# GpSimd's share of the weight splits, the context squares of the first norm, and the pieces of the first modulation weights in a two-layer block

## The chip, the cores and the metric

The kernel runs on one core of a Trainium2 chip. The metric is the time of one execution on the device in microseconds; the median of several runs counts. A core has five engines that work in parallel on instruction streams of their own: TensorE (PE in the profile; its weight loads are PEld), VectorE (DVE), ScalarE (ACT), GpSimd (POOL) and SyncE (SP). SP, ACT and POOL also issue DMA transfers; SPq, ACTq and POOLq are those queues.

## What is computed

A block of two layers over 512 tokens of 1024 channels (`x`) and 256 context tokens (`ctx`). Each layer has three parts: a half feed-forward network, a mixer, another half feed-forward network. Every part normalises its input, modulates it with terms computed from a condition vector `c`, and adds its gated output to the residual.

```python
def rms_norm(x, g):
    xf = x.astype(jnp.float32)
    y = xf * lax.rsqrt(jnp.mean(jnp.square(xf), axis=-1, keepdims=True) + EPS)
    return (y * g.astype(jnp.float32)).astype(x.dtype)
def modulate(x, g, shift, scale):
    return rms_norm(x, g) * (1.0 + scale) + shift
def swiglu(h, w_in, w_out):
    a, b = jnp.split(h @ w_in, 2, axis=-1)
    return (jax.nn.silu(a) * b) @ w_out
def macaron_half_ffn(x, g, shift, scale, gate, w_in, w_out):
    return x + 0.5 * gate * swiglu(modulate(x, g, shift, scale), w_in, w_out)
```

The mixer of layer 0 combines neighbourhood attention and an mLSTM, that of layer 1 is a spatial gating unit. The context takes part in layer 0 up to its mixer. `w_mod` holds, for each layer, nine modulation terms as 1024 x 1024 matrices. All of it is float32.

## The kernel before

Channels lie on the 128 partitions: `xT` is 128 x 8 x 512, eight channel tiles (k = 0 to 7) of 512 tokens, and `cT` the same for the context. To reach float32 accuracy with TensorE's faster format, each operand of a large product is split into a high and a low half, and a product is three matmuls: high by high, low by high, high by low.

**The weight stream.** All large weights come through one `Stream` object, `W`, in the order of use, 128 x 1024 tiles numbered from 0. `load` starts the transfer `raw` on SP, in a ring of three buffers. `prep` lets ScalarE cast `raw` to the high half `whi` (L83) and subtracts to get the low half `wlo` (L84), four buffers each. The subtraction, called the split here, runs on VectorE, except for the tile numbers in the set `W.pool`, which go to GpSimd:

```python
(nc.gpsimd if i in self.pool else nc.vector).tensor_tensor(lo, r, hi.bitcast(F32), ALU.subtract)
...
W.pool.update(range(6))
for i in mark:
    W.pool.update(range(i - 4, i + 4))
```

`mark` holds the tile numbers at which one part ends and the next begins, so the set has the first six tiles and four on either side of five hand-overs: 62 to 69, 98 to 105, 164 to 171, 230 to 237 and 278 to 285, 46 in all.

**The hand-overs.** They are numbered 1 to 5 here: feed-forward 00 to mixer, mixer to feed-forward 01, 01 to 10, 10 to gating, gating to 11 (first digit the layer, second the part). The last products of a part (`pl...`) go in two halves of 256 tokens. Each adds its tile to the residual (L306, VectorE); ScalarE squares it (`sq`, L229) and VectorE adds the square to `nacc` (L230). After eight tiles TensorE sums `nacc` over the partitions (`st_x`), ScalarE takes the root (`nr_x`, L239) and loads a table ahead of the next function (L215), VectorE takes the reciprocal (L242), TensorE broadcasts it (`bc_x`), and for each k VectorE makes `nt` (L255), ScalarE the high half `hx..h` (L256) and VectorE the low half `hx..l` (L257) of the next part's input. The first products of the next part (`pa`, `pb`) follow k by k. Names carry the part: `hx10l` and `nacc_x10` belong to feed-forward 10, the context's are `hc`, `nacc_c`, `st_c`.

**The start.** Feed-forward 00 can't begin before its modulation terms are there. `load_mod` fetches 1 MB for each k (`wmk`, L572) as four transfers, in which a piece of 512 bytes goes to each place; `mod_products` multiplies it with the condition (`pm`), VectorE copies the result (`mr`, L616), `mod_columns` turns it into columns (`pcol`) and computes gain `G` and shift `S`, and `modulated` makes `hx00` for this k (L637 to L639), which `x_products` uses (`st`). The norm of `x` is `norm_start` (squares on ScalarE, seven adds into `sacc` on VectorE, L596), and it is called a second time, for the context, at k = 4 of the loop, ahead of `x_products(4)`. Behind the loop `ctx_modulated` makes `hc00` for the context (L643 to L645) and `ctx_products` uses it (`stc`).

**Work in the background.** The modulation terms needed later are not products but sums on VectorE: `mod_task` loads 512 KB (`wm`, L153) by GpSimd's queue into a ring of three buffers, and VectorE accumulates (`macc`, L159 the first, L161 the rest), for the first terms twice per load, once for each condition vector. `mp0`, which holds these buffers, takes the place in memory of the start's tiles.

**What sets the order.** The program is written in Python with a library that gives each engine one instruction stream, worked off in order; the library moves instructions against the written order by the dependencies, by the buffers of its tile pools (an instruction that reuses a buffer waits for the last reader) and by its own estimate of when a result is ready. `gtiles` gives out the buffers of the gated activations `gx` and `gc`; `spacer` is a tile with a small memset on GpSimd that shifts what comes behind it in memory.

Of the kernel before, what the change touches and what calls it, by code (L numbers as in the profile page):

```python
# [37 lines left out]
def block_kernel(ctx: ExitStack, tc: tile.TileContext, T: dict, out: bass.AP, stop: str = ""):  # L38
    nc = tc.nc
# [55 lines left out]
    W = Stream()  # L95
# [335 lines left out]
    def ffn(l, s, cur, nxt, gxf, gcf, bgsteps, side, first=None, left=0):  # L431
        nm = f"{l}{s}"
        hx, hc = cur.hx, cur.hc
        bgn[0] = bgsteps
        nslot = 6 if hc else 8
        gx = gc = None
        with tc.tile_pool(name=f"g{nm}", bufs=1, side=side, reuse_waits="tile") as gp:
            def glu(pa, pb, n, gh, gl, nme):
                sl = gp.tile([P, 512], F32, tag="silu", name=f"sl{nme}", bufs=2)[:, :n]
                nc.scalar.activation(halved(sl), inorder(pa), AF.Silu)  # L440
                nc.vector.tensor_tensor(halved(sl), halved(sl), inorder(pb), ALU.mult)  # L441
                nc.scalar.copy(gh, sl)
                last = nc.vector.tensor_tensor(gl, sl, gh.bitcast(F32), ALU.subtract)
                if not hc:
                    pace[0] = last

            def gtiles(f):
                e = f % nslot if hc or f < 18 else f"z{f}"
                if not hc and f == 18:
                    spacer(gp, 192, f"padz{nm}")  # L450
                g = [gp.tile([P, 512], F32R, tag=f"gx{e}{i}", name=f"gx{nm}{f}{i}") for i in range(2)]
                if hc:
                    if f < nslot:
                        spacer(gp, 192, f"padgc{f}")
                    g += [gp.tile([P, 256], F32R, tag=f"gc{e}{i}", name=f"gc{nm}{f}{i}") for i in range(2)]
                    if f < nslot:
                        spacer(gp, 64, f"padge{f}")
                if not hc and f == NF - 1:
                    spacer(gp, 64, f"padze{nm}")
                return g  # L460

            gs = {f: gtiles(f) for f in range(2)}
            if first:
                for f in range(2):
                    pab, pc = first[f]
                    glu(pab[0], pab[1], 512, gs[f][0], gs[f][1], f"st{f}")
                    glu(pc[:, :256], pc[:, 256:], 256, gs[f][2], gs[f][3], f"stc{f}")
            else:
                us = list(zip(*[[W.next(), W.next()] for hf in range(2)]))
            for t0, t1 in () if first else HALVES:  # L470
                for f in range(2):
                    pab = bank(f"pa{nm}{f}{t0}"), bank(f"pb{nm}{f}{t0}")
                    for k in range(KD):
                        if (t0, f) == (0, 0) and k in (5, 7):
                            cur.go()
                        for ab in range(2):
                            w = pick(us[f][k // 4], slice(None), k % 4, slice(ab * P, (ab + 1) * P))
                            product(pab[ab][:, :256], w, pick(hx, slice(None), k, slice(t0, t1)), k == 0, k == 7)
                    glu(pab[0][:, :256], pab[1][:, :256], 256, gs[f][0][:, t0:t1], gs[f][1][:, t0:t1], f"{nm}{f}{t0}")
            bg.step(2 * bgsteps)  # L480
            for kind, f in ffn_order(l, s):
                if kind == "o":
                    if gx is None:
                        bg.finish()
                        gx, gc = gxf(), gcf() if hc else None
                    out_op(f"{nm}{f[0]}", [gs.pop(i) for i in range(*f)], (f[1] - f[0]) // 4, gx, gc)
                elif f > 1:
                    u = [W.next(), W.next()]
                    g = gs[f] = gtiles(f)
                    pab = bank(f"pa{nm}{f}"), bank(f"pb{nm}{f}")  # L490
                    pc = bank(f"pc{nm}{f}") if hc else None
                    for hf in range(2):
                        for ab in range(2):
                            for kk in range(4):
                                k = hf * 4 + kk
                                w = pick(u[hf], slice(None), kk, slice(ab * P, (ab + 1) * P))
                                x = pick(hx, slice(None), k)
                                if hc:
                                    product2(pab[ab], pc[:, ab * 256:(ab + 1) * 256], w, x, pick(hc, slice(None), k),
                                             k == 0, k == 7, k == 0 and ab == 0, k == 7 and ab == 1)  # L500
                                else:
                                    product(pab[ab], w, x, k == 0, k == 7)
                    glu(pab[0], pab[1], 512, g[0], g[1], f"{nm}{f}")
                    if hc:
                        glu(pc[:, :256], pc[:, 256:], 256, g[2], g[3], f"{nm}{f}c")
                    bg.step(bgsteps)
            bg.need(left)
            cur.close()
            nxt.open()
            out_c(f"{nm}c", [gs[16], gs[17]], gx, gc)  # L510
            out_last(f"{nm}l", [gs[i] for i in range(18, NF)], gx, nxt, gc)
# [11 lines left out]
    mark = []  # L523
# [23 lines left out]
    mark.append(len(W.aps))  # L547
    stream_ffn(1, 1)
    W.pool.update(range(6))
    for i in mark:  # L550
        W.pool.update(range(i - 4, i + 4))


    cpool = ExitStack()
# [4 lines left out]
    sp = spx.enter_context(tc.tile_pool(name="sp", bufs=1, side="right"))  # L559
# [7 lines left out]
    def load_mod(i):  # L567
        k0, k1 = MODK[i]
        t = sp.tile([P, KD, 2, (k1 - k0) * P], F32, tag="wmk", name=f"wmk{i}", bufs=5)
        for h in range(2):  # L570
            for j in range(2):
                nc.sync.dma_start(t[:, 4 * h:4 * h + 4, j], T["w_mod"][0, 512 * h:512 * h + 512, j * D + k0 * P:j * D + k1 * P]  # L572
                                  .rearrange("(k p) c -> p k c", p=P))
        wmk.append(t)

    for k in range(0, KD, 2):
# [9 lines left out]
        load_mod(i)  # L586
    warm(AF.Sqrt, cs[:, 0, 0:1])

    def norm_start(nn, n):
        st = aux(f"sts{n}")  # L590
        acc = sp.tile([P, N], F32, tag="sacc", name=f"sacc{n}", bufs=1)[:, :n]
        for k in range(KD):
            sq = sp.tile([P, N], F32, tag="ssq", name=f"ssq{n}{k}", bufs=4)[:, :n] if k else acc
            nc.scalar.activation(sq, nn.x[:, k], AF.Square)
            if k:
                nc.vector.tensor_tensor(acc, acc, sq, ALU.add)  # L596
        for c in range(n // P):
            mm(st[:, 2 * c:2 * c + 2], acc[:, c * P:(c + 1) * P], ones, True, True)
        r = tp.tile([P, 8], F32, tag="nrs", name=f"nrs{n}", bufs=1)[:, :n // 64]
        nc.scalar.activation(r, st[:, :n // 64], AF.Sqrt, bias=epst, scale=1.0 / D)  # L600
        if n == NCX:
            warm(AF.Silu, r[:, 0:1])
        nc.vector.reciprocal(r, r)
        bc = aux(f"bcx{n}")
        for c in range(n // P):
            mm(bc[:, c * P:(c + 1) * P], r[:, 2 * c:2 * c + 1].to_broadcast([P, P]), ident, True, True)
        return bc[:, :n]
# [12 lines left out]
    for k in range(5):  # L620
        mm(junk, ones[:, 0:1].to_broadcast([P, P]), xT[:, k], True, True)
    mrs = {0: mod_products(0)}
    bcx = norm_start(s00.nx, N)
    xn = sp.tile([P, KD, N], F32, name="xn")
    s00.open()

    def start():
# [44 lines left out]
        def x_products(k):  # L672
            for f in range(2):
                for ab in range(2):
                    w = pick(us[f][k // 4], slice(None), k % 4, slice(ab * P, (ab + 1) * P))
                    product(pab[f][ab], w, pick(hx, slice(None), k), k == 0, k == 7)
# [642 lines left out]
def layout(i):  # L1319
    a = {}  # L1320
    a["xT"] = i["x"][0].T.reshape(KD, P, N).transpose(1, 0, 2)
    a["cT"] = i["ctx"][0].T.reshape(KD, P, NCX).transpose(1, 0, 2)
    a["cc"] = np.stack([i["c"][0], i["c_ctx"]]).reshape(2, KD, P).transpose(2, 0, 1)
    a["w_mod"] = i["w_mod"]
    a["b_mod"] = i["b_mod"].reshape(2, 9, KD, P).transpose(3, 0, 1, 2)
    a["norm_g"] = i["norm_g"].reshape(2, 3, KD, P).transpose(3, 0, 1, 2)
    a["final_g"] = i["final_g"].reshape(KD, P).T
# [74 lines left out]
```

## Time and profile before

| | |
|---|---|
| median of three runs | 2307.08 us (2306.27 to 2308.08) |
| the profiled execution | 2307.41 us |
| its span in the trace | 2305.6 us, so 1.8 us around it |
| TensorE busy | 2246.3 us, 97% of the span |
| VectorE, ScalarE, GpSimd busy | 56%, 34%, 11% |
| splits on VectorE / on GpSimd | 302 / 46 |

Times are in microseconds from the start of the span. A row of a group names source line, engine, operation and tiles with buffer numbers left out, how often it occurs, its busy time and the mean of one in nanoseconds, and the idle time of that engine ahead of it with what ended it. A row of the timeline has start, duration, engine, line and operation; several equal instructions in a row are merged (x3), their duration being that from the first start to the last end. PEclk is TensorE's granted clock as a share of its full one; 0.50 is its level of 1.2 GHz, 1.00 that of 2.4 GHz.

### The profile page before, as it was taken

The numbers are of one execution on the slowest core, as the hardware profiler recorded it, in microseconds if no ns is written. First come the engines' busy times: TensorE is split into PE (matmuls) and PEld (weight loads), VectorE is DVE, ScalarE is ACT, GpSimd is POOL, SyncE is SP. The second block draws the span as 40 slices with busy tenths as digits, with TensorE's granted clock in tenths as the row PEclk, the third lists the DMA queues.
The fourth block names the chain that finished last, engine by engine and source line by source line (L and its number), as shares of the span: only waits on it lengthen the run. The fifth ranks groups of instructions, "written<-read, shape, count | busy, mean of one in ns | idle before, by whom it ended". The sixth has DMA issues, their size and how long they took to land.

```text
span 2305.6 us, 31899 instructions
## 1 busy us (share of the span) xinstructions
PE 2246.3 (97%) x12926; PEld 1989.7 (86%) x12926; DVE 1284.2 (56%) x2045; ACT 779.7 (34%) x1283; POOL 262.8 (11%) x300
## 2 busy tenths in 40 slices
PE   7999999999999999999999999999999999999998
PEld 4999999999878977888888898888878888988887
DVE  5996653327556447766574766433536756433336
ACT  3322122124354356532323432322335424323222
POOL 2212120002030033100010301000300003000000
PEclk8999999999999989999999999999999999999999
DMA  8566561221122231165564356333242322333231
GB/s 268 175 201 196 167 185 65 70 68 52 63 83 65 65 119 62 65 210 192 173 211 155 111 174 210 101 101 101 92 146 93 99 92 74 101 100 108 94 110 65
DMA packets 95347, 281.33 MB, mean 122 GB/s; under 512 B 11024, under 2 KB 29632, under 8 KB 94816
## 3 DMA queue, kind: packets, MB, share of 16 engines
q1 hardware_dynamic: 69648, 196.18, 25.7%
q0 software_dynamic: 22960, 77.99, 11.3%
q10 hardware_dynamic: 2592, 5.13, 0.7%
q8 instruction: 101, 1.65, 0.3%
q14 instruction: 46, 0.38, 0.1%
HBM read 274.95 MB, written 6.00 MB: 122 GB/s over the span
## 4 chain that ended last, share of the span: by engine, by line
PE 88%; DVE 6%; issue 3%; ACT 1%; DMA 1%; POOL 0%; ACTq 0%; DVEq 0%; POOLq 0%
PE pa L108 19%; PE pb L108 19%; PE po L108 14%; PE pc L108 4%; PE su L108 4%; PE sv L108 4%; PE posg L108 3%; PE poc L108 2%; PE O L108 1%; PE tva L108 1%; PE nS L108 1%; PE st L108 1%; PE pomx L108 1%; PE fqa L108 1%; PE pl11l L108 1%
## 5 line engine op out<-in xcount | busy, mean ns | idle before, releaser
L83 ACT CAST whi<-raw 128x1024 fp32r<-128x1024 f32 x348 | 364.8, 1049 | 919.1 <-PE pb L108 330.4
L84 DVE TENSOR_TENSOR wlo<-raw,whi 128x1024 fp32r<-128x1024 f32 x302 | 370.1, 1226 | 399.6 <-ACT whi L83 383.7
L108 PE MATMUL po<-gx,whi 128*128 128x512 f32 x1024 | 305.4, 380 | 0.0
L441 DVE TENSOR_TENSOR sl<-sl,pb 128x512 f32<-128x512 f32 (+1 forms) x92 | 60.0, 652 | 272.0 <-PE pb L108 182.1
L108 PEld LDWEIGHTS po<-gx,whi 128*128 128x128 f32 x1024 | 183.7, 189 | 24.0
L108 PE MATMUL po<-gx,wlo 128*128 128x512 f32 x512 | 194.4, 380 | 0.0
L84 POOL TENSOR_TENSOR wlo<-raw,whi 128x1024 fp32r<-128x1024 f32 (+1 forms) x46 | 109.8, 2388 | 598.7 <-ACT whi L83 585.1
L161 DVE SCALAR_TENSOR_TENSOR macc<-wm,cs,macc 128x1024 f32<-128x1024 f32 x133 | 168.3, 1280 | 10.5 <-DMA wm<-in_w_mod 9.4
L153 POOL DMA_DIRECT2D wm<-in_w_mod x128 | 68.1, 532 | 573.9 <-DVE macc L161 368.7
L306 DVE SCALAR_TENSOR_TENSOR xT<-po,gate,xT 128x512 f32<-128x512 f32 x80 | 59.8, 748 | 95.9 <-PE po L108 95.8
L440 ACT ACTIVATE sl<-pa 128x512 f32<-128x512 f32 (+1 forms) x92 | 52.3, 569 | 174.3 <-PE pa L108 174.3
L108 PEld LDWEIGHTS po<-gx,wlo 128*128 128x128 f32 x512 | 97.2, 190 | 10.2
L108 PE MATMUL pc<-hc00l,whi 128*128 128x256 f32 x320 | 88.0, 275 | 0.0
L108 PE MATMUL pc<-hc00h,whi 128*128 128x256 f32 x320 | 87.3, 273 | 0.0
L108 PE MATMUL pc<-hc00h,wlo 128*128 128x256 f32 x320 | 87.2, 273 | 0.0
L108 PE MATMUL pa<-hx12l,whi 128*128 128x512 f32 (+1 forms) x192 | 70.5, 367 | 3.1 <-DVE hx12l L257 3.1
L108 PE MATMUL pa<-hx10l,whi 128*128 128x512 f32 (+1 forms) x192 | 70.2, 366 | 3.1 <-DVE hx10l L257 3.1
L108 PE MATMUL pa<-hx02l,whi 128*128 128x512 f32 (+1 forms) x192 | 70.2, 366 | 2.8 <-DVE hx02l L257 2.8
L108 PE MATMUL pa<-hx02h,whi 128*128 128x512 f32 (+1 forms) x192 | 70.3, 366 | 0.1
L108 PE MATMUL pa<-hx12h,whi 128*128 128x512 f32 (+1 forms) x192 | 70.3, 366 | 0.0
L108 PE MATMUL pa<-hx10h,whi 128*128 128x512 f32 (+1 forms) x192 | 70.1, 365 | 0.0
L108 PE MATMUL pa<-hx12h,wlo 128*128 128x512 f32 (+1 forms) x192 | 70.0, 365 | 0.0
(561 smaller groups left out, 5893.6 us busy)
## 6 DMA issues: line engine op xcount, KB each, us to landing
raw<-in_ffn_in SPq DMA_DIRECT2D x176, 512.0 KB, 3.3
wm<-in_w_mod POOLq DMA_DIRECT2D x128, 512.0 KB, 4.6
raw<-in_ffn_out SPq DMA_DIRECT2D x64, 512.0 KB, 3.3
raw<-in_mix_in SPq DMA_DIRECT2D x26, 512.0 KB, 3.2
wmk<-in_w_mod SPq DMA_DIRECT2D x32, 256.0 KB, 5.4
raw<-in_ffn_last SPq DMA_DIRECT2D x16, 512.0 KB, 3.3
raw<-in_sg_v SPq DMA_DIRECT2D x16, 512.0 KB, 3.4
raw<-in_sg_u SPq DMA_DIRECT2D x16, 512.0 KB, 3.5
```

The source lines that it names most:

```text
L83: nc.scalar.copy(hi, r)
L84: (nc.gpsimd if i in self.pool else nc.vector).tensor_tensor(lo, r, hi.bitcast(F32), ALU.subtract)
L108: lastmm[0] = nc.tensor.matmul(o, lhsT, rhs, start=start, stop=stop)
L153: ins = nc.gpsimd.dma_start(wt, T["w_mod"][l, k * P:(k + 1) * P, j * D:(j + 1) * D])
L161: nc.vector.scalar_tensor_tensor(acc[v], wt, cs[:, v, k:k + 1], acc[v], ALU.mult, ALU.add)
L306: nc.vector.scalar_tensor_tensor(xs, inorder(o), g[:, k:k + 1], xs, ALU.mult, ALU.add)
L440: nc.scalar.activation(halved(sl), inorder(pa), AF.Silu)
L441: nc.vector.tensor_tensor(halved(sl), halved(sl), inorder(pb), ALU.mult)
```

## The change

There are four edits. `W.pool` keeps only the first six tiles; the 40 splits around the hand-overs run on VectorE. `norm_start` is taken apart: `square_start` does one square and one add on a given engine. The norm of `x` calls it with VectorE as before; the context's eight squares are now written two at a time at k = 3 to 6 of the loop, with their adds on GpSimd, and its `norm_start` at k = 6 behind `x_products(6)`. The host lays out the first modulation weights as `w_mod0`, so that `load_mod` makes two transfers of 512 KB per k, with 4 KB in one piece, instead of four of 256 KB. And `gtiles` has neither spacers nor buffers of their own for the steps from 18 on.

```diff
             def gtiles(f):
-                e = f % nslot if hc or f < 18 else f"z{f}"
-                if not hc and f == 18:
-                    spacer(gp, 192, f"padz{nm}")
+                e = f % nslot
...
-                    if f < nslot:
-                        spacer(gp, 192, f"padgc{f}")
...
     W.pool.update(range(6))
-    for i in mark:
-        W.pool.update(range(i - 4, i + 4))
...
         for h in range(2):
-            for j in range(2):
-                nc.sync.dma_start(t[:, 4 * h:4 * h + 4, j], T["w_mod"][0, 512 * h:512 * h + 512, j * D + k0 * P:j * D + k1 * P]
-                                  .rearrange("(k p) c -> p k c", p=P))
+            nc.sync.dma_start(t[:, 4 * h:4 * h + 4], T["w_mod0"][k0, h])
...
+    sacc = {}
+
+    def square_start(nn, n, k, eng):
+        if k == 0:
+            sacc[n] = sp.tile([P, N], F32, tag="sacc", name=f"sacc{n}", bufs=1)[:, :n]
+        sq = sp.tile([P, N], F32, tag="ssq", name=f"ssq{n}{k}", bufs=4)[:, :n] if k else sacc[n]
+        nc.scalar.activation(sq, nn.x[:, k], AF.Square)
+        if k:
+            eng.tensor_tensor(sacc[n], sacc[n], sq, ALU.add)
+
+    def norm_start(n):
         st = aux(f"sts{n}")
-        acc = sp.tile([P, N], F32, tag="sacc", name=f"sacc{n}", bufs=1)[:, :n]
-        for k in range(KD):
-            sq = sp.tile([P, N], F32, tag="ssq", name=f"ssq{n}{k}", bufs=4)[:, :n] if k else acc
-            nc.scalar.activation(sq, nn.x[:, k], AF.Square)
-            if k:
-                nc.vector.tensor_tensor(acc, acc, sq, ALU.add)
+        acc = sacc[n]
...
         for k in range(KD):
-            if k == 4:
-                bc = norm_start(s00.nc, NCX)
             x_products(k)
+            if 3 <= k < 7:
+                for i in range(2 * k - 6, 2 * k - 4):
+                    square_start(s00.nc, NCX, i, nc.gpsimd)
+            if k == 6:
+                bc = norm_start(NCX)
```

What this moves on the engines is seen at three places. First VectorE at hand-over 3, the end of the first half's modulation; the numbers at the ends of names tell tiles apart (`pl01l07256` is channel tile 7 of the second half, `sq_x10_7_256` its square). Before:

```order
L257 SCALAR_TENSOR_TENSOR hx10l_11681<-nt_x10_0_7_12023,mod_1_0_0_9945,hx10h_11680 128x256
L230 TENSOR_TENSOR nacc_x10_256_11937<-nacc_x10_256_11937,sq_x10_4_256_12045 128x256
L306 SCALAR_TENSOR_TENSOR xT_82<-pl01l06256_12065,gate_0_2_0_10025,xT_82 128x256
L230 TENSOR_TENSOR nacc_x10_256_11937<-nacc_x10_256_11937,sq_x10_5_256_12062 128x256
L306 SCALAR_TENSOR_TENSOR xT_82<-pl01l07256_12082,gate_0_2_0_10025,xT_82 128x256
L230 TENSOR_TENSOR nacc_x10_256_11937<-nacc_x10_256_11937,sq_x10_6_256_12079 128x256
L230 TENSOR_TENSOR nacc_x10_256_11937<-nacc_x10_256_11937,sq_x10_7_256_12096 128x256
L242 RECIPROCAL nr_x10_256_12166<-nr_x10_256_12166 128x4
```

The same place on VectorE after:

```order
L257 SCALAR_TENSOR_TENSOR hx10l_11637<-nt_x10_0_7_11979,mod_1_0_0_9905,hx10h_11636 128x256
L230 TENSOR_TENSOR nacc_x10_256_11893<-nacc_x10_256_11893,sq_x10_5_256_12018 128x256
L306 SCALAR_TENSOR_TENSOR xT_82<-pl01l07256_12038,gate_0_2_0_9985,xT_82 128x256
L230 TENSOR_TENSOR nacc_x10_256_11893<-nacc_x10_256_11893,sq_x10_6_256_12035 128x256
L84 TENSOR_TENSOR wlo170_12064<-raw170_11726,whi170_12063 128x1024
L230 TENSOR_TENSOR nacc_x10_256_11893<-nacc_x10_256_11893,sq_x10_7_256_12052 128x256
L84 TENSOR_TENSOR wlo171_12070<-raw171_11732,whi171_12069 128x1024
L242 RECIPROCAL nr_x10_256_12122<-nr_x10_256_12122 128x4
```

Two splits now stand around the last sum; two more (`wlo168`, `wlo169`) stand ahead of the first reciprocal and behind the first `nt`.

Second, GpSimd at the start of feed-forward 00. Before, without the memsets in between:

```order
L84 TENSOR_TENSOR wlo3_247<-raw3_140,whi3_246 128x1024
...
L153 DMA wm0_2_0_792<-in_w_mod 128x1024
L153 DMA wm0_2_1_798<-in_w_mod 128x1024
L84 TENSOR_TENSOR wlo4_253<-raw4_242,whi4_252 128x1024
L84 TENSOR_TENSOR wlo5_259<-raw5_244,whi5_258 128x1024
L153 DMA wm0_2_2_802<-in_w_mod 128x1024
```

GpSimd after; the seven adds of the context's squares stand where the dots are:

```order
L84 TENSOR_TENSOR wlo3_231<-raw3_132,whi3_230 128x1024
...
L84 TENSOR_TENSOR wlo4_237<-raw4_226,whi4_236 128x1024
L84 TENSOR_TENSOR wlo5_243<-raw5_228,whi5_242 128x1024
L153 DMA wm0_2_0_768<-in_w_mod 128x1024
L153 DMA wm0_2_1_774<-in_w_mod 128x1024
L153 DMA wm0_2_2_778<-in_w_mod 128x1024
```

All loads of `wm0_2` moved behind the two splits.

Third, VectorE a little later, from the first gating product of `st`; `macc0_2_0` and `macc0_2_1` are the sums for the two condition vectors. Before:

```order
L443 TENSOR_TENSOR gx0001_757<-slst0_772,gx0000_756 128x512
L159 TENSOR_SCALAR macc0_2_0_794<-wm0_2_0_792,cs_84 128x1024
L159 TENSOR_SCALAR macc0_2_1_796<-wm0_2_0_792,cs_84 128x1024
L161 SCALAR_TENSOR_TENSOR macc0_2_0_794<-wm0_2_1_798,cs_84,macc0_2_0_794 128x1024
L161 SCALAR_TENSOR_TENSOR macc0_2_1_796<-wm0_2_1_798,cs_84,macc0_2_1_796 128x1024
L84 TENSOR_TENSOR wlo6_819<-raw6_250,whi6_818 128x1024
L441 TENSOR_TENSOR slstc0_777<-slstc0_777,stc0_268 128x256
```

After, from the last of the six gating products on:

```order
L443 TENSOR_TENSOR gc0011_747<-slstc1_763,gc0010_746 128x256
L161 SCALAR_TENSOR_TENSOR macc0_2_1_772<-wm0_2_1_774,cs_84,macc0_2_1_772 128x1024
L161 SCALAR_TENSOR_TENSOR macc0_2_0_770<-wm0_2_2_778,cs_84,macc0_2_0_770 128x1024
...
L161 SCALAR_TENSOR_TENSOR macc0_2_0_770<-wm0_2_5_790,cs_84,macc0_2_0_770 128x1024
L161 SCALAR_TENSOR_TENSOR macc0_2_1_772<-wm0_2_5_790,cs_84,macc0_2_1_772 128x1024
L84 TENSOR_TENSOR wlo6_795<-raw6_234,whi6_794 128x1024
L84 TENSOR_TENSOR wlo7_801<-raw7_240,whi7_800 128x1024
```

`wlo6` stood behind four accumulations and stands behind twelve.

## Rows read from the trace of the kernel before

**Rows 1.** The page's part 4: the chain that ended last, by engine.

```profile
PE 88%; DVE 6%; issue 3%; ACT 1%; DMA 1%; POOL 0%; ACTq 0%; DVEq 0%; POOLq 0%
```

**Rows 2.** Waits of TensorE: product, what it waited for: us in total, times, longest.

```profile
PE st_x L108 <- DVE nacc_x L230: 12.2, 5, 4.2
...
PE pa L108 <- DVE hx10l L257: 3.1, 3, 1.3
...
PE pcol L108 <- DVE mr L616: 2.7, 1, 2.7
```

**Rows 3.** Busy time by stretch: PE, PEld, DVE, ACT, POOL, then PEclk, DMA share, GB/s.

```profile
560.00:590.00 30.00, 23.94 (x168) 23.32 (x168) 23.33 (x43) 14.38 (x30) 10.11 (x9) 0.83 0.29 94
955.00:975.00 20.00, 15.11 (x112) 14.16 (x111) 15.84 (x35) 9.66 (x22) 6.73 (x8) 0.91 0.43 158
1310.00:1330.00 20.00, 14.92 (x111) 14.12 (x110) 15.60 (x34) 9.57 (x21) 5.00 (x5) 0.91 0.24 79
1665.00:1690.00 25.00, 18.71 (x75) 15.12 (x74) 15.63 (x35) 10.71 (x22) 4.24 (x3) 0.86 0.54 190
1940.00:1960.00 20.00, 14.95 (x98) 14.15 (x97) 14.17 (x30) 8.90 (x19) 4.93 (x3) 0.83 0.25 80
```

**Rows 4.** The same view, two stretches behind idle time, at the start and hand-over 3.

```profile
43.30:50.10 6.80, 5.73 (x26) 3.10 (x27) 2.79 (x11) 0.81 (x1) 0.00 (x0) 0.50 0.66 257
...
1323.30:1326.70 3.40, 3.40 (x19) 3.40 (x18) 0.87 (x3) 1.57 (x4) 0.00 (x0) 0.50 0.00 0
```

**Rows 5.** Timelines at hand-over 3, of GpSimd, VectorE and ScalarE.

```profile
1310.39 2.35 POOL L84 TENSOR_TENSOR wlo<-raw,whi 128x1024 fp32r<-128x1024 f32 x1 [0.23 <-ACT whi L83]
...
1303.62 2.23 DVE L230 TENSOR_TENSOR nacc_x<-nacc_x,sq_x 128x256 f32<-128x256 f32 x1
...
1306.79 0.43 DVE L230 TENSOR_TENSOR nacc_x<-nacc_x,sq_x 128x256 f32<-128x256 f32 x1 [0.55 <-ACT sq_x L229]
...
1308.70 4.72 DVE L257 SCALAR_TENSOR_TENSOR hx10l<-nt_x,mod,hx10h 128x256 fp32r<-128x256 f32 x3
...
1314.86 1.26 DVE L257 SCALAR_TENSOR_TENSOR hx10l<-nt_x,mod,hx10h 128x256 fp32r<-128x256 f32 x3
...
1321.21 0.43 DVE L230 TENSOR_TENSOR nacc_x<-nacc_x,sq_x 128x256 f32<-128x256 f32 x1 [0.21 <-ACT sq_x L229]
...
1322.62 1.28 ACT L215 ACT_TABLE_LOAD   x1
```

**Rows 6.** The page's costliest groups: the splits on VectorE and on GpSimd.

```profile
L84 DVE TENSOR_TENSOR wlo<-raw,whi 128x1024 fp32r<-128x1024 f32 x302 | 370.1, 1226 | 399.6 <-ACT whi L83 383.7
...
L84 POOL TENSOR_TENSOR wlo<-raw,whi 128x1024 fp32r<-128x1024 f32 (+1 forms) x46 | 109.8, 2388 | 598.7 <-ACT whi L83 585.1
```

**Rows 7.** Timeline at the start: GpSimd, VectorE, TensorE around the copy of `mr4`.

```profile
37.87 2.37 POOL L84 TENSOR_TENSOR wlo<-raw,whi 128x1024 fp32r<-128x1024 f32 x1 [1.88 <-ACT whi L83]
...
38.45 5.25 DVE L596 TENSOR_TENSOR sacc<-sacc,ssq 128x256 f32<-128x256 f32 x7 [0.87 <-ACT ssq L594]
...
44.09 1.01 PE L108 MATMUL pcol<-sel,mr 128*128 128x2 f32 x4 [2.71 <-DVE mr L616]
```

**Rows 8.** Timelines and one tile's answer between 64 and 96: products, splits, accumulations.

```profile
64.65 0.27 PE L108 MATMUL stc<-hc00h,whi 128*128 128x256 f32 x1
...
70.60 5.16 POOL L84 TENSOR_TENSOR wlo<-raw,whi 128x1024 fp32r<-128x1024 f32 x2 [8.45 <-ACT whi L83]
...
79.29 1.21 DVE L84 TENSOR_TENSOR wlo<-raw,whi 128x1024 fp32r<-128x1024 f32 x1
...
85.35 7.26 DVE L161 SCALAR_TENSOR_TENSOR macc<-wm,cs,macc 128x1024 f32<-128x1024 f32 x6
...
91.75 0.38 PE L108 MATMUL pa<-hx00h,wlo 128*128 128x512 f32 x1
...
L159 DVE TENSOR_SCALAR macc<-wm,cs x2: 742/1804/2865, 73.5 to 76.2; 128x1024 f32<-128x1024 f32 x2
...
DMA to landing us min/median/max: 4.1/4.6/7.3
```

More of the change, by code (lines that the diff above doesn't have):

```diff
@@ L447, in gtiles @@
             def gtiles(f):
-                e = f % nslot if hc or f < 18 else f"z{f}"
-                if not hc and f == 18:
-                    spacer(gp, 192, f"padz{nm}")
+                e = f % nslot
                 g = [gp.tile([P, 512], F32R, tag=f"gx{e}{i}", name=f"gx{nm}{f}{i}") for i in range(2)]
                 if hc:
-                    if f < nslot:
-                        spacer(gp, 192, f"padgc{f}")
                     g += [gp.tile([P, 256], F32R, tag=f"gc{e}{i}", name=f"gc{nm}{f}{i}") for i in range(2)]
[L456 to L459, printed above, removed]
                 return g
@@ L587, in block_kernel @@
     warm(AF.Sqrt, cs[:, 0, 0:1])
-    def norm_start(nn, n):
-        st = aux(f"sts{n}")
-        acc = sp.tile([P, N], F32, tag="sacc", name=f"sacc{n}", bufs=1)[:, :n]
-        for k in range(KD):
-            sq = sp.tile([P, N], F32, tag="ssq", name=f"ssq{n}{k}", bufs=4)[:, :n] if k else acc
-            nc.scalar.activation(sq, nn.x[:, k], AF.Square)
-            if k:
-                nc.vector.tensor_tensor(acc, acc, sq, ALU.add)
+    sacc = {}
[7 more added lines that the diff above has]
+    def norm_start(n):
+        st = aux(f"sts{n}")
+        acc = sacc[n]
         for c in range(n // P):
@@ L622, in block_kernel @@
     mrs = {0: mod_products(0)}
-    bcx = norm_start(s00.nx, N)
+    for k in range(KD):
+        square_start(s00.nx, N, k, nc.vector)
+    bcx = norm_start(N)
     xn = sp.tile([P, KD, N], F32, name="xn")
@@ L1324, in layout @@
     a["w_mod"] = i["w_mod"]
+    a["w_mod0"] = i["w_mod"][0, :, :2 * D].reshape(2, 4, P, 2, KD, P).transpose(4, 0, 2, 1, 3, 5)
     a["b_mod"] = i["b_mod"].reshape(2, 9, KD, P).transpose(3, 0, 1, 2)
```

## The prediction

> **What bounds the kernel now.** I read the chain that ended last first: 88% of it is TensorE [rows 1], so time is won only where TensorE stands still or runs slowly. The waits of TensorE come next [rows 2]. Their longest entry is the statistics product of a norm, `st_x`, behind VectorE's sums of squares: 12.2 us in five waits. The products `pa` behind `hx10l`, the low half of a modulated input, have 3.1 us in three waits; `hx12l` (3.1) and `hx02l` (2.8) repeat it. `pcol` behind `mr` is one wait of 2.7. No row of that list names `wmk`, the first modulation weights. The table of the five hand-overs then shows where the waits lie [rows 3]: TensorE is busy 23.94 of 30, 15.11, 14.92 and 14.95 of 20, and 18.71 of 25 us, so 6.1, 4.9, 5.1, 5.0 and 6.3 us stand idle, 27.4 together. Its granted clock there is 0.83, 0.91, 0.91, 0.83 and 0.86; shortfall times length is 5.1, 1.8, 1.8, 3.4 and 3.5, another 15.6. Behind the idle stretches there are some at 0.50, the level of 1.2 GHz, with TensorE busy throughout in the second row shown [rows 4]. The price of a hand-over is thus 11, 7, 7, 8.4 and 10 us, 43 in all.
>
> The timeline of hand-over 3 tells why VectorE is late there [rows 5]. The sum `nacc_x` takes 0.43 us at 1306.79 and 2.23 at 1303.62. Three `hx10l` take 4.72 us at 1308.70 and 1.26 at 1314.86. The long ones, and only they, fall together with splits on GpSimd, the last of the three with that from 1310.39 to 1312.74. I read this as: a VectorE instruction whose operands all lie in SBUF doesn't finish while a GpSimd split runs. The last sum ends at 1321.64, `st_x` follows, then a square root, a table load of 1.28 us that stands ahead of the reciprocal, and the second half of the hand-over.
>
> **The change part by part.** *Splits to VectorE.* Forty splits go from 2.39 us on GpSimd to 1.23 on VectorE (1.14 in a run) [rows 6]. At hand-over 3, VectorE loses 4.7 − 1.3 = 3.4 us of holding at the three `hx10l`, 1.8 at the first sum and some 0.7 later, 5.9; it gains four splits, 4.6. One lies where VectorE idles ahead of the reciprocal and one behind the last sum, so two, 2.3, are on the way to that sum. I laid the new order out with durations of the rows: first half's `nt`/`hx10l` done by 1315.4, the last residual at 1316.2, `wlo170` 1316.5 to 1317.7, last sum at 1318.2 in place of 1321.6, `wlo171` until 1319.2. TensorE's first product stays at 1310.86, since the second residual products end there. Its order now has the products of `w169` ahead of those with `wlo170`, so it reaches `wlo170` at 1317.0 and waits 0.6; the statistics cost nothing; the reciprocal, behind the table load, comes at 1320.4, a wait of 0.5; the second half waits 0.5 for its first `hx10l`. That is 1.6 idle instead of 5.1. With idle in crumbs I expect the 1.8 of clock to come back mostly. Gain 5.1 at best, 2 if the clock falls all the same and VectorE, now fuller, gives back 1.5 in the second half; I take 4.5.
> Hand-over 5 has the same shape, but a larger clock loss (3.4): I take 4, between 2 and 7. Hand-over 2 has it too, but two activation table loads change places with the square root, 1.28 each [rows 5]: 3, between 0 and 5. At hand-over 4 one wait of 4.2 for `nacc_x` is nearly all of it [rows 2]; its sums are freed of GpSimd, but two splits come ahead of them: 3, between 0 and 7. At hand-over 1 the context norm follows the second norm, and `wlo68` and `wlo69` now stand between the last context sums, 2.3 us on the chain: 2.5 of 11, between 0 and 7. Together −17, between −31 and −4.
>
> *Context squares to GpSimd.* Before, seven adds occupy VectorE for 5.25 us from 38.45, the first behind a split of GpSimd until 40.24; the copy of `mr4` stands behind them and TensorE waits 2.71 for it at 44.09 [rows 7]. Now the copy comes at once, and the low clock from 43.30 to 50.10 (0.50) [rows 4] should shorten: up to 2.7 + 2.1. Against it, the context norm ends later, with `bcx256` two products ahead of the first context product: one `sttc`, high and low half of some 0.45 to 0.5 each stand open, 1.2. An add on GpSimd isn't in the trace; by columns it is 2.39 / 4 = 0.6, at most a whole split, 2.4, and seven make 4.2 to 17; four steps of TensorE at about 3 us hide the first and not the second. Nearest is the former, the same operation. It may hold short VectorE work by 0.6 a piece. Sum −3, between −4.5 and +3.
> A rule speaks against this part: the Trainium skill, GPSIMD Engine Reference, section Engine selection, sends elementwise work on a tile to VectorE, since GpSimd is some two times slower. The split's two rows agree (2388 against 1226 ns). By the rule alone the seven adds would be a loss of some 1.3 us, 7 × (0.60 − 0.42); by the rows they leave an engine that TensorE is waiting for, and TensorE decides.
>
> *What the new GpSimd order costs.* This is the loss that the diff doesn't show. Before, two loads of the next modulation's weights (`wm0_2`) are issued ahead of `wlo4` and `wlo5`; now all stand behind them. Count from the first context product, T = 64.65 [rows 8]. GpSimd's two splits end at T + 11.1 before; the casts that they wait for stand behind the context's high halves in both orders, and laid out they come to the same offset, so I keep it; a `wm` lands 4.1 to 7.3 us later (4.6 typical; 4.3 for the first on an idle queue), so the first accumulation starts at T + 15.4 instead of T + 8.8. VectorE's order now has two first products of 0.7, ten accumulations of 1.21 and six gating products (some 2.6) from there to `wlo6`; before, `wlo6` stood behind four of them and was done at 80.50, T + 15.9. Sum: 15.4 + 1.4 + 12.1 + 2.6 + 1.2 = T + 32.7. TensorE wants `wlo6` at 91.75, T + 27.1. So 11 us of slack turn into a wait of 5.6. If the clock falls after it, up to 3 more. I take +6, between 0 (a shorter queue than I think) and +9 (landing at 7.3). Behind it VectorE is ahead again.
>
> *4 KB pieces, spacers, slots.* Sixteen loads instead of thirty-two, larger pieces. TensorE waits for no `wmk` [rows 2], so a faster stream ends earlier for nobody: 0, between −1.5 and +0.5. Memsets of about 0.1 us vanish from an idle engine, and `gx` slots are reused after eight steps, with the old readers long done: 0. If that cover were gone, it would show as a wait of `gx`.
>
> Sum: −17 − 3 + 6 + 0 = −14 against the profiled execution, 2307.4 (span 2305.6 and 1.8 around it). The median of the runs is 2307.1, 0.3 lower. Forecast 2293.
>
> **The rivals.** *B, VectorE becomes the bound at hand-overs.* The holding goes, but TensorE only waits elsewhere, at `wlo170` and its like, with the clock falling as before. For it: VectorE is busy 15.60 of 20 us already at hand-over 3 [rows 3]. Against it: my layout leaves it 1.6 us of waits. A gain of 1 each: −5 − 3 + 6 = −2, 2305.
> *C, casts stop VectorE.* A split on GpSimd that waits for ScalarE's cast holds nobody; on VectorE, which works in order, the sums and the `hx` behind it wait too. VectorE's own splits have idle time of 399.6 us ahead of them, 383.7 of it ended by `whi` [rows 6]. In my layout the casts are 2 us early. Each us of TensorE waiting that they cause costs one at each of five hand-overs; from 14 / 5 = 2.8 us on, the whole passes from gain to loss; at 4 us it is −17 + 20 = +3 at the hand-overs, with −3 and +6 at the start +6 in all: 2313. Against it: ScalarE is busy less than half there, 9.57 of 20 us [rows 3].
> *D, no wait for `wlo6`.* If `wm` comes earlier or TensorE's order has more to do, +6 falls to 0, and the start and clock come at their better ends: 2285.
> *E, the pieces count*, because the first hidden tiles come sooner: 3 us more, 2290.
> *The change doesn't do what it says*: if the long sums have another cause than GpSimd, the splits only lengthen the chain by 2.3 each; that ends near C, 2320.
>
> **How the numbers follow.** Forecast 0.58, its own range 2285 to 2301; D 0.12; E 0.06; B 0.13; C with the last 0.11. Measurement here tells 0.2%, 4.6 us, from no change: faster is below 2302.5, slower above 2311.7. The forecast, D and E lie below, 0.76; with a little of B 0.77. Most of B is the same, 0.12; C is slower, 0.11. The range leaves out C and the lowest tail of D: 2281 to 2306.
>
> **What would show it.** At each hand-over no `nacc_x` or `hx` over 0.6 us, TensorE's idle at 3 falling to about 2 and the clock near 0.98; at the start no wait of `pcol` for `mr`; a wait of about 5 us at the first product with `wlo6`, some 27 us after the first context product, with VectorE busy accumulating. I am wrong if hand-overs keep their idle under another name, if TensorE waits for `whi` through VectorE, or if the sums stay long with GpSimd silent.

## The result and the profile after

The changed kernel takes 2278.2 us, median of four runs (2277.3 to 2279.7), against 2307.2 before: a ratio of 0.9875, 95% interval 0.9858 to 0.9892, 29 us faster. The forecast was 2293 with a range of 2281 to 2306. The direction was right; the gain is twice what was forecast and lies outside the range.

The page after, part 4 (share of the ended-last chain by engine), and then the waits of TensorE (product, what it waited for: us in total, times, longest):

```profile
PE 90%; DVE 4%; issue 4%; ACT 1%; DMA 1%; POOL 0%; DVEq 0%; POOLq 0%; ACTq 0%
```

```profile
PE pa L108 <- DVE wlo L84: 5.3, 1, 5.3
...
PE pa L108 <- ACT hx02h L256: 1.6, 1, 1.6
...
PE bc_x L108 <- DVE nr_x L242: 1.4, 1, 1.4
...
PE pcol L108 <- DVE mr L609: 0.5, 1, 0.5
PE st_x L108 <- DVE nacc_x L230: 0.4, 1, 0.4
```

Against [rows 2], `st_x` behind `nacc_x` went from 12.2 to 0.4 us, the waits behind `hx..l` are gone, and `pcol` behind `mr` went from 2.7 to 0.5. At the top stands one that wasn't there, a split that `pa` waits for. The five hand-overs, in the columns of [rows 3] (length, busy PE, PEld, DVE, ACT, POOL, PEclk, DMA share, GB/s):

```profile
565.00:595.00 30.00, 29.56 (x254) 29.13 (x253) 26.02 (x65) 19.26 (x42) 0.40 (x4) 1.00 0.30 95
952.00:972.00 20.00, 16.91 (x132) 16.34 (x131) 15.88 (x38) 12.86 (x25) 0.00 (x0) 0.91 0.42 158
1305.00:1325.00 20.00, 19.75 (x168) 18.94 (x167) 17.96 (x42) 11.97 (x26) 0.00 (x0) 1.00 0.20 60
1653.00:1678.00 25.00, 23.84 (x117) 20.47 (x116) 19.21 (x40) 15.51 (x29) 0.00 (x0) 1.00 0.38 128
1921.00:1941.00 20.00, 19.75 (x168) 18.95 (x168) 17.41 (x40) 11.87 (x25) 0.00 (x0) 1.00 0.22 75
```

Four of five have lost nearly all their idle time (0.4, 0.25, 1.2 and 0.25 us are left) and run at full clock; hand-over 2 keeps 3.1 us of idle time and 0.91. The same product in both traces dates the gains (start in us; the last column is what the difference changed by since the row above):

| first product of its kind | before | after | difference | since the row above |
|---|---|---|---|---|
| `pa` with `wlo4`, behind the start | 76.03 | 73.62 | −2.4 | −2.4 |
| `pl00l`, ahead of hand-over 1 | 535.49 | 540.56 | +5.1 | +7.5 |
| `S`, in the mixer | 648.78 | 643.70 | −5.1 | −10.1 |
| `pa` with `hx02h`, in hand-over 2 | 955.65 | 952.55 | −3.1 | +2.0 |
| `pa` with `hx10h`, in hand-over 3 | 1310.86 | 1305.79 | −5.1 | −2.0 |
| `sv` with `hx11h`, in hand-over 4 | 1664.97 | 1653.53 | −11.4 | −6.4 |
| `pa` with `hx12h`, in hand-over 5 | 1940.92 | 1920.94 | −20.0 | −8.5 |
| `st_xf`, at the end | 2286.37 | 2258.61 | −27.8 | −7.8 |

The gain is the hand-overs' (−34.8 in all); the start gives 2.4, feed-forward 00 takes 7.5, and the mixer takes 2.0, part of it clock: the 7 us behind its longest gap ran at 1.00 before and at 0.76 in this trace, though the gap is as long. The 2.4 of the start isn't clear of what single traces differ by: three kernels of the experiments (e1, e9, e10) have the start of the kernel before, instruction for instruction, and reach the product with `wlo4` 2.3 us later, 1.0 and 2.3 us earlier than it.

### The profile page after: what moved, and what is told of

Its sections match the earlier page's. It is cut to its first block, busy times and chain, and to the rows that moved or that the text cites. A ratio compares the mean times of both kernels' runs of the same rounds, so it can differ in the third digit from the quotient of the medians.

```text
span 2277.9 us, 31832 instructions
## 1 busy us (share of the span) xinstructions
PE 2237.2 (98%) x12926; PEld 1980.4 (87%) x12926; DVE 1292.4 (57%) x2078; ACT 780.2 (34%) x1285; POOL 172.6 (8%) x249
## 4 chain that ended last, share of the span: by engine, by line
PE 90%; DVE 4%; issue 4%; ACT 1%; DMA 1%; POOL 0%; DVEq 0%; POOLq 0%; ACTq 0%
PE pa L108 19%; PE pb L108 19%; PE po L108 14%; PE pc L108 4%; PE su L108 4%; PE sv L108 3%; PE posg L108 3%; PE poc L108 2%; PE O L108 1%; PE tva L108 1%; PE nS L108 1%; PE S L108 1%; PE pomx L108 1%; PE fqa L108 1%; PE pl11l L108 1%
## 5 line engine op out<-in xcount | busy, mean ns | idle before, releaser
L84 DVE TENSOR_TENSOR wlo<-raw,whi 128x1024 fp32r<-128x1024 f32 x342 | 423.4, 1239 | 401.9 <-ACT whi L83 384.7
L440 ACT ACTIVATE sl<-pa 128x512 f32<-128x512 f32 (+1 forms) x92 | 52.3, 568 | 178.0 <-PE pa L108 174.9
L108 PE MATMUL pb<-hx02h,whi 128*128 128x512 f32 (+1 forms) x192 | 70.1, 365 | 0.1
L108 PE MATMUL pa<-hx02h,wlo 128*128 128x512 f32 (+1 forms) x192 | 69.7, 363 | 0.0
L108 PE MATMUL pa<-hx10h,wlo 128*128 128x512 f32 (+1 forms) x192 | 69.5, 362 | 0.1
```

Of the source, the lines that this page charges most:

```text
L108: lastmm[0] = nc.tensor.matmul(o, lhsT, rhs, start=start, stop=stop)
```

## The experiments

Theory: a subtraction on GpSimd holds VectorE's instructions whose operands lie in SBUF, and that alone cost TensorE idle time and clock at the hand-overs; the new wait, for `wlo6`, is one of order. Rivals: the new order of the instructions made the gain, or the missing spacers, or the context squares and pieces have a part in it.

### The splits alone (e1_splits_only)

The kernel before without the three other edits:

```diff
     W.pool.update(range(6))
-    for i in mark:
-        W.pool.update(range(i - 4, i + 4))
```

> Only the first edit on the kernel before: the forty splits around the hand-overs go to VectorE; context squares, pieces, spacers and slots stay. Theory (the splits on GpSimd held VectorE, and that alone cost TensorE the idle time and the low clock at the hand-overs): hand-overs 1, 3, 4, 5 give what the changed kernel shows, 10.1 + 6.4 + 8.5 + 7.8 = 32.8 us, hand-over 2 gives 4 to 6 since no table load changes place in this order, nothing at the start, and no wait at wlo6, since the order there stays as before: 2307 - 37 = about 2270, under the changed kernel. Rival (the new order of several edits together, or the missing spacers, made the hand-overs short): 2290 to 2305.

Measured: 2268.7 us, ratio 0.9838 (0.9821 to 0.9854), 9.5 below the whole change by the medians and 8.5 by the ratios to the kernel before. Hand-overs 2 and 3 in columns as above:

```profile
950.00:970.00 20.00, 19.75 (x168) 18.95 (x167) 17.09 (x39) 11.91 (x25) 0.00 (x0) 1.00 0.25 79
1298.00:1318.00 20.00, 19.75 (x168) 18.94 (x167) 17.53 (x40) 11.78 (x26) 0.00 (x0) 1.00 0.21 65
```

Hand-over 2 is now as clean as hand-over 3. One edit of four makes more than the whole gain, and the other three together cost some 9 us beside it.

### The holding put back (e2_dup)

The changed kernel with idle work for GpSimd:

```diff
                 (nc.gpsimd if i in self.pool else nc.vector).tensor_tensor(lo, r, hi.bitcast(F32), ALU.subtract)
+                if i in self.dup:
+                    fr, fh = [x.rearrange("p a b -> p (a b)") if len(r.shape) == 3 else x for x in (r, hi)]
+                    m = fr.shape[1] // 4
+                    for c in range(4):
+                        cc = slice(m * c, m * c + m)
+                        d = wp.tile([P, m], F32, tag="dup", name=f"dup{i}_{c}", bufs=1)
+                        nc.gpsimd.tensor_tensor(d, fr[:, cc], fh[:, cc].bitcast(F32), ALU.subtract)
```

> The changed kernel, and on GpSimd, for the same forty tiles, the same subtraction once more into a scratch tile that nobody reads, in four pieces of 256 columns. VectorE, TensorE and ScalarE keep the changed kernel's instructions in its order. Theory (a GpSimd subtraction holds VectorE's instructions whose operands lie in SBUF): VectorE has the splits and the holding, some 5 to 6 us a hand-over, and TensorE's idle time and low clock return: 2300 to 2320, with nacc_x and hx..l of over 1 us where GpSimd works. Rival (the gain came from the order, or from a split ending sooner): within 3 us of 2278.

Measured: 2311.5 us, ratio to before 1.0015 (1.0005 to 1.0026): the whole gain is gone. Timelines of GpSimd and VectorE at hand-over 3 (start, duration, idle time ahead in brackets), among them two of GpSimd's pieces by themselves, then that hand-over and the next in the columns by stretch:

```profile
1311.96 15.40 POOL L92 TENSOR_TENSOR dup<-raw,whi 128x256 f32<-128x256 f32 x16 [9.44 <-issue]
...
1315.45 1.59 POOL L92 TENSOR_TENSOR dup<-raw,whi 128x256 f32<-128x256 f32 x1
...
1317.12 0.79 POOL L92 TENSOR_TENSOR dup<-raw,whi 128x256 f32<-128x256 f32 x1
```

```profile
1315.06 1.39 DVE L85 TENSOR_TENSOR wlo<-raw,whi 128x1024 fp32r<-128x1024 f32 x1
...
1317.25 0.95 DVE L265 SCALAR_TENSOR_TENSOR hx10l<-nt_x,mod,hx10h 128x256 fp32r<-128x256 f32 x1
...
1320.20 2.30 DVE L265 SCALAR_TENSOR_TENSOR hx10l<-nt_x,mod,hx10h 128x256 fp32r<-128x256 f32 x3
1322.42 1.25 DVE L263 SCALAR_TENSOR_TENSOR nt_x<-xT,G,bc_x 128x256 f32<-128x256 f32 x3
1323.60 0.58 DVE L238 TENSOR_TENSOR nacc_x<-nacc_x,sq_x 128x256 f32<-128x256 f32 x1
1324.10 2.68 DVE L265 SCALAR_TENSOR_TENSOR hx10l<-nt_x,mod,hx10h 128x256 fp32r<-128x256 f32 x3
```

```profile
1318.00:1338.00 20.00, 16.87 (x114) 15.72 (x113) 15.83 (x32) 8.87 (x19) 8.58 (x11) 0.83 0.30 106
1673.00:1698.00 25.00, 19.86 (x84) 16.63 (x83) 19.28 (x40) 12.27 (x25) 8.00 (x12) 0.86 0.34 119
```

Three `hx10l` take 2.30 and 2.68 us instead of 1.27; `nt`, whose operand `bc_x` lies in PSUM, stays at 1.25 under the same pieces. The ends of the two engines' instructions, laid side by side, show how: each of the 30 `hx..l` and 24 sums that began while a piece had 0.2 us or more to run ended 0.28 to 0.29 us behind that piece, as the held ones of the kernel before do behind the splits. The `hx10l` at 1317.25 is one (the piece ends at 1317.91, it at 1318.20). It goes the other way too: each of the 30 pieces that began under a split on VectorE ended 0.58 to 0.60 us behind that split, as the one at 1315.45 does, and took 1.5 to 1.8 us instead of the 0.73 to 0.80 of most.

The order of the instructions is that of the changed kernel, and GpSimd's results go nowhere, so order and a split's own end are excluded. One thing else differs: the pieces read `raw` and `whi`, so these buffers come free later, and some casts on ScalarE wait for a piece. The next experiment has the same waits (us in total, times, longest; this one first):

```profile
ACT whi L84 <- POOL dup L92: 8.0, 5, 1.9
```

```profile
ACT whi L84 <- POOL dup L92: 11.3, 8, 1.7
```

With more waiting of that kind the other one loses 4 to 6 us, not 33, so the buffers aren't the cause: the holding is. The Trainium skill, GPSIMD Engine Reference, section Specifications, says that GpSimd shares its SBUF interfaces with VectorE and contends with VectorE's instructions that have two SBUF inputs; these rows agree, and add how long each waits.

### A copy in place of the subtraction (e8_dup_copy)

```diff
-                        nc.gpsimd.tensor_tensor(d, fr[:, cc], fh[:, cc].bitcast(F32), ALU.subtract)
+                        nc.gpsimd.tensor_copy(d, fh[:, cc].bitcast(F32))
```

> As e2, with a plain copy of the high half on GpSimd in place of the subtraction, in the same four pieces of 256 columns into the scratch tile: one SBUF operand read instead of two. Order of VectorE, TensorE and ScalarE as in the changed kernel. Theory A (any GpSimd instruction that works on SBUF holds VectorE for its duration): above the changed kernel in proportion to the copies' time; with pieces of 0.3 to 0.9 us, 2288 to 2311. Theory B (only an instruction with two SBUF inputs holds): within 3 us of 2278.

Measured: 2284.3 us, ratio 0.9894 (0.9879 to 0.9908), so 6 above the changed kernel by the medians and 4 by the ratios: between the two forecasts. GpSimd's group with two of its pieces, and VectorE's instructions beside those two:

```profile
L92 POOL COPY dup<-whi 128x256 f32<-128x256 f32 (+1 forms) x160 | 98.2, 614 | 756.8 <-ACT whi L84 749.3
...
1301.60 1.39 POOL L92 COPY dup<-whi 128x256 f32<-128x256 f32 x1 [0.28 <-ACT whi L84]
...
1303.06 0.47 POOL L92 COPY dup<-whi 128x256 f32<-128x256 f32 x1
```

```profile
1301.51 1.23 DVE L85 TENSOR_TENSOR wlo<-raw,whi 128x1024 fp32r<-128x1024 f32 x1
...
1303.19 0.61 DVE L265 SCALAR_TENSOR_TENSOR hx10l<-nt_x,mod,hx10h 128x256 fp32r<-128x256 f32 x1
```

A copy holds like a subtraction, until it ends: the `hx10l` at 1303.19 ends 0.27 us behind the copy (1303.80 and 1303.53), and so, within 0.02, do all 18 `hx..l` and 16 sums that began while a copy had 0.2 us or more to run. It is held in turn: the copy at 1301.60 ends 0.26 us behind the split on VectorE, at 1.39 us instead of 0.40. So theory B is wrong, and of theory A the mechanism is right and the price too high. A copy that isn't held mostly takes 0.40 to 0.47 us, a subtraction 0.73 to 0.80, so less of each is left to wait for. Added up from the traces over `hx..l`, sums and splits (against 0.48, 0.43 and 1.23 us when free), VectorE is held for some 25 to 30 us in the kernel before, 23 in e2 and 5 to 6 in this one.

### Which splits (e9_early_on_gpsimd, e10_late_on_gpsimd)

The kernel before, with half of the splits moved:

```diff
 e9
-        W.pool.update(range(i - 4, i + 4))
+        W.pool.update(range(i - 4, i))
 e10
-        W.pool.update(range(i - 4, i + 4))
+        W.pool.update(range(i, i + 4))
```

> The kernel before, with the four splits behind each hand-over's mark (the next part's first four) moved to VectorE, and the four ahead of it left on GpSimd: 20 splits moved instead of 40, the other three edits left out. Theory (holding costs only where TensorE waits for VectorE, and that is the stretch in which the next part's first four splits run; the four ahead of it run some 10 to 30 us earlier, while VectorE has time): as e1, 2268 to 2271. Rival (any split on GpSimd near a hand-over costs): halfway, 2285 to 2295.

> The complement: the next part's first four splits stay on GpSimd, the four ahead of the mark go to VectorE. Theory: the hand-overs keep their idle time and low clock, 2304 to 2308. Rival: halfway, 2285 to 2295.

Measured: e9 2270.7 us, ratio 0.9834 (0.9819 to 0.9849); e10 2306.3, ratio 0.9996 (0.9986 to 1.0006). First the last early split of hand-over 3 in e9 and a gating product on VectorE under an earlier one (1261.17 to 1263.54), then that hand-over in e9 and in e10:

```profile
1271.95 2.37 POOL L84 TENSOR_TENSOR wlo<-raw,whi 128x1024 fp32r<-128x1024 f32 x1 [2.79 <-ACT whi L83]
...
1261.70 2.38 DVE L443 TENSOR_TENSOR gx<-sl,gx 128x512 fp32r<-128x512 f32 x1 [0.41 <-ACT gx L442]
```

```profile
1294.00:1314.00 20.00, 19.70 (x167) 18.88 (x166) 16.90 (x39) 11.88 (x26) 0.00 (x0) 1.00 0.25 80
```

```profile
1308.00:1328.00 20.00, 14.93 (x112) 14.14 (x111) 15.39 (x31) 9.51 (x20) 5.74 (x5) 0.91 0.24 79
```

Twenty splits make all of it. The twenty others, done on GpSimd some 20 us ahead of the critical stretch, hold VectorE too (this gating product takes 2.38 us instead of 0.68), but TensorE isn't waiting for it there, and moving them alone does nothing.

### The context squares alone (e5_ctx_only)

The second edit on the kernel before, as in the diff ahead of the prediction.

> Only the second edit on the kernel before: the context's squares two at a time with their adds on GpSimd, the context norm behind x_products(6). The loads of wm stand behind wlo4 and wlo5 on GpSimd in this order too, but no accumulation stands ahead of wlo6, and spacers, slots and the splits at the hand-overs are as before. Theory: the wait of pcol for mr4 and the low clock behind it go, -2.4 to -3 to the first gating products; the late loads make the first background sum late, and TensorE waits for it (mt behind msum) 3 to 4 us where it waited 0.7, with low clock behind it; hand-overs unchanged: 2307 + 2 = 2309, between 2305 and 2311. Rival (the late loads are harmless as long as wlo6 is early): 2304.

Measured: 2309.3 us, ratio 1.0009 (0.9999 to 1.0018). Two rows of TensorE's waits:

```profile
PE st_x L108 <- DVE nacc_x L230: 12.4, 5, 4.3
...
PE mt L108 <- DVE msum L167: 3.1, 1, 3.1
```

The hand-overs are as before. The wait for `mr4` (2.7) is gone, and in its place stands one of 3.1 for the first background sum, whose weights are loaded late. This edit alone is worth nothing.

### The pieces alone (e6_pieces_only)

The third edit on the kernel before.

> Only the third edit on the kernel before: sixteen loads of 512 KB with 4 KB in a piece for the first modulation weights. Theory (the stream ends some 4 us earlier, but TensorE waits for VectorE there and not for wmk): 2306 to 2307, within 0.1% of before, with the transfers of the start ending near 41 instead of 46 us. Rival (the pieces count): 2303 or less.

Measured: 2306.9 us, ratio 1.0001 (0.9990 to 1.0012): the same. The start in the columns by stretch, the last two being DMA share and GB/s, first of this kernel and then of the kernel before:

```profile
20.00:32.00 12.00, 11.32 (x76) 5.99 (x76) 7.67 (x24) 2.56 (x3) 2.49 (x2) 0.86 1.02 420
...
40.00:46.00 6.00, 2.96 (x16) 1.85 (x16) 3.59 (x13) 1.07 (x2) 0.00 (x0) 0.85 0.19 71
```

```profile
20.00:32.00 12.00, 11.34 (x65) 5.83 (x65) 7.50 (x25) 1.84 (x3) 2.36 (x1) 0.74 1.03 348
...
40.00:46.00 6.00, 3.29 (x30) 1.55 (x28) 4.27 (x15) 1.72 (x4) 0.24 (x1) 0.78 1.11 366
```

The transfers run at 420 instead of 348 GB/s and are nearly through by 40 us, where they were at full load before; no product waited for them. Four other kernels with the pieces of before (e1, e5, e9, e10) move 373 to 377 GB/s from 20 to 32 us, so the trace of the kernel before is at the low end; and the transfers themselves are larger too, 512 instead of 256 KB. The Trainium skill, DMA: Bandwidth & Descriptors, section Specifications, sets the smallest piece for full rate at 512 bytes; here the stream with pieces of 512 bytes moved 10 to 17% less than that with 4 KB, and the measurement decides.

### Spacers, and the loads behind the splits (e3_spacers_back, e4_pool4, e7_spacers_pool4)

Three kernels on the changed one: e3 puts the lines of `gtiles` back as they were, e4 has

```diff
-    W.pool.update(range(6))
+    W.pool.update(range(4))
```

and e7 has both.

> The changed kernel with the spacers and the separate slots of gtiles put back as they were before; the other three edits stay. In its order no accumulation stands ahead of wlo6, and no activation table load changes place at hand-over 2. Theory (the wait of 5.3 us at wlo6, 7.5 with the low clock behind it, and some 4 us at hand-over 2 are matters of order that the fourth edit brought): 2278 - 7.5 - 4 = about 2267. Rival (spacers and slots change nothing that counts, and the wait comes from the late loads of wm alone): 2274 to 2279.

> The changed kernel with wlo4 and wlo5 on VectorE too, so that the loads of wm don't stand behind them on GpSimd; in its order no accumulation stands ahead of wlo6. Hand-overs as in the changed kernel. Theory (the wait at wlo6 is twelve accumulations that waited for late loads): it goes, with the low clock behind it, 7.5 us: 2271. Rival (VectorE, which is busy without a pause there, only passes the wait on to wlo7, wlo8 or the gating products): 2276 to 2279.

> The changed kernel with the spacers and slots of before and with wlo4 and wlo5 on VectorE: experiments e3 and e4 in one. In its order the loads of wm stand right behind the context's adds, no accumulation ahead of wlo6, and no table load changes place at hand-over 2. Theory (both causes are separate and add up): 8.4 us at the start of feed-forward 00, as in e4, and 4.4 at hand-over 2, less 1.1 at hand-over 4, as in e3: 2278 - 12 = 2266, the fastest. Rival (the background sums are the bound there and find another place to make TensorE wait): 2269 to 2272.

Measured: e3 2272.3 us, ratio to before 0.9858 (0.9843 to 0.9873); e4 2274.0, 0.9862 (0.9847 to 0.9877); e7 2269.1, 0.9833 (0.9815 to 0.9852). In all three the wait for `wlo6` is gone. In e3, TensorE waits elsewhere, with low clock behind it (waits, then a stretch of e3):

```profile
PE mt L108 <- DVE msum L167: 3.8, 1, 3.8
```

```profile
105.00:113.00 8.00, 6.11 (x26) 5.26 (x27) 8.00 (x13) 2.35 (x4) 1.06 (x2) 0.59 0.40 133
```

By the same comparison of products e3 saves 1.4 of the 7.5 us between 60 and 120 us, and e4, whose loads come earlier, 6.9, of which it gives back 2.4 when VectorE makes TensorE wait at 335 us; e7 saves 7.1 and gives back 1.0. At hand-over 2, e3 and e7 gain 4.4 us and e4 nothing: with the slots of before, the activation tables are not changed to and fro. In the changed kernel ScalarE loads three within 5.5 us there:

```profile
959.57 1.28 ACT L440 ACT_TABLE_LOAD   x1
...
961.27 1.28 ACT L239 ACT_TABLE_LOAD   x1
...
963.78 1.28 ACT L215 ACT_TABLE_LOAD   x1
```

The first serves a gated activation (L440) that has slipped ahead of the norm's root (L239), the second the root, the third what comes behind it; before there is one, and with the slots put back (e3) one again. Both causes add up in e7, though its median is 3 us above what was expected; e7, e1 and e9 can't be told apart (2267 to 2274 in single runs). Each of them beats both kernels.

## Why the prediction was wrong, step by step

**The splits: the mechanism was right and the term too small**, −17 against −34.8, and it is the term that put the time outside the range. (As I worded it, the reading of [rows 5] is a little too wide: the reciprocal of 128x4, all of it in SBUF, took its 0.18 us at 1303.31 in the middle of the split from 1303.20 to 1305.57. The sums and `hx..l`, with two tensors from SBUF, are held.) At hand-over 3, which I had laid out, take 5.07 us off the layout's times, as TensorE was that much ahead by then. VectorE and TensorE in the trace after:

```profile
1304.93 1.27 DVE L257 SCALAR_TENSOR_TENSOR hx10l<-nt_x,mod,hx10h 128x256 fp32r<-128x256 f32 x3
...
1311.45 1.22 DVE L84 TENSOR_TENSOR wlo<-raw,whi 128x1024 fp32r<-128x1024 f32 x1
1312.58 0.42 DVE L230 TENSOR_TENSOR nacc_x<-nacc_x,sq_x 128x256 f32<-128x256 f32 x1
...
1315.61 0.18 DVE L242 RECIPROCAL nr_x<-nr_x 128x4 f32<-128x4 f32 x1 [1.47 <-ACT junk L215]
```

```profile
1312.30 0.28 PE L108 MATMUL pb<-hx10l,whi 128*128 128x256 f32 x1
1312.72 0.38 PE L108 MATMUL pa<-hx10h,wlo 128*128 128x256 f32 x1
...
1313.16 0.51 PE L108 MATMUL st_x<-ones,nacc_x 128*128 128x2 f32 x4
```

`wlo170` was laid out for 1311.4 and began at 1311.45; the last sum was to end at 1313.1 and ended at 1313.00; the reciprocal was to come at 1315.3 and came at 1315.61. VectorE's side thus held to 0.3 us. TensorE's side didn't: it reached the product with `wlo170` 0.5 us later than laid out and waited 0.3 instead of 0.6, and the waits of 0.5 for the reciprocal and of 0.5 for the second half shrank to what overlapping products cover. Idle is 0.25 instead of 1.6, and no low clock follows, where I let it come back "mostly": 6.4 instead of 4.5, above the 5.1 that I called the best.

**Hand-overs 1, 4 and 5 were not laid out, and there the error is largest**: 2.5, 3 and 4 against 10.1, 8.5 and 7.8, all three beyond the upper bounds that I gave them. I knew the price (11, 10, 8.4) and gave a part of it because splits stand ahead of the sums. That overlooks what the two sides cost: a split adds 1.14 us at its place in VectorE's queue, while on GpSimd it costs the time for which VectorE is held (0.7 to 2.2 us at each held instruction of the kernel before), and then the clock that TensorE loses behind its wait. Of their price of 29 us I booked 9.5 and 26.4 came; no row gave a reason for so deep a cut.

**Hand-over 2** was expected at −3 and gave −2.0, by the table loads that I had named; e3 shows that they come with the fourth edit, which I had set at nothing. That step was wrong: the slots cost no wait of `gx`, but they changed the library's order.

**The wait for `wlo6`** came as worked out. GpSimd, VectorE and TensorE after; the first context product is at 61.84 here:

```profile
68.37 4.91 POOL L84 TENSOR_TENSOR wlo<-raw,whi 128x1024 fp32r<-128x1024 f32 x2 [22.25 <-ACT whi L83]
73.23 1.60 POOL L153 DMA_DIRECT2D wm<-in_w_mod  x3
```

```profile
77.88 0.75 DVE L159 TENSOR_SCALAR macc<-wm,cs 128x1024 f32<-128x1024 f32 x1 [4.04 <-DMA wm<-in_w_mod]
...
82.94 10.85 DVE L161 SCALAR_TENSOR_TENSOR macc<-wm,cs,macc 128x1024 f32<-128x1024 f32 x9
93.70 2.36 DVE L84 TENSOR_TENSOR wlo<-raw,whi 128x1024 fp32r<-128x1024 f32 x2
```

```profile
94.97 0.80 PE L108 MATMUL pa<-hx00h,wlo 128*128 128x512 f32 x1 [5.26 <-DVE wlo L84]
```

The first accumulation starts 16.0 us behind the first context product (15.4 expected), `wlo6` is there some 33.1 behind it (32.7), and TensorE waits 5.26 us (5.6). With the clock behind it (0.56 from 95.0 to 101.8) and 0.7 given back at the first `mt`, it cost 7.5 against +6.

**The context squares** were set at −3 and gave −2.4 in the one trace, which isn't clear of the spread at the start; the wait of `pcol` fell from 2.7 to 0.5 (the same in e5), with no low clock between 40 and 61 us; their bill is the wait for late weights, which I had booked apart. An add on GpSimd took 0.73 us, not 0.6. What decided was neither the add's own time nor the freed VectorE, but what the moved work did to the loads on GpSimd's queue (e5: no gain).

**The pieces** were set at 0, and e6 says so.

Of the rivals, B (VectorE becomes the bound) and C (casts stop it) didn't come: hand-over 3 has VectorE busy 17.96 of 20 us and TensorE idle 0.25. D's condition failed, E's too. That the long sums have another cause than GpSimd is excluded by e1 and e2.

## What to carry to other kernels

Don't give GpSimd work on SBUF in a stretch where another engine waits for VectorE: it isn't free help. A subtraction or a copy there stops VectorE's instructions with two SBUF inputs for as long as it runs; the same splits some 20 us earlier cost nothing. When a cause has been found and priced, take it away in the sum whole, the clock that falls behind a wait included, and lay out every place that it touches, or leave the range open to its full price. A change of slots or spacers that moves no work can still move table loads and queue heads, so the order after is read for it.

## What the runs showed of the hardware

A GpSimd subtraction or copy holds a VectorE instruction with two SBUF tensors until it ends (a sum of 256 columns goes from 0.43 to 2.2 us beside a subtraction of 1024), and one with a tensor in PSUM not at all; the held one ends 0.28 us behind the subtraction, 0.27 behind the copy. A VectorE split holds GpSimd likewise (a piece of 0.73 us takes 1.6). The clock behind a gap isn't a fixed price: the gap ahead of `S` is 2.8 us before and 2.7 after, and the 7 us behind it ran at 1.00 and at 0.76. Single times of one kernel spread by some 6 us; in e1's profiled execution, its slowest, the clock was at 0.52 from 44.2 to 57.8 us, where the kernel before shows it low for 7 us behind the same wait.
